# One decoder layer in fp32 on one core: the embedding operand in another order, and its weights' second parts by accumulating transfers

## The chip, the cores and the metric

The kernel runs on one core of one Trainium2 chip. The core has five engines that run side by side: TensorE (PE, with a separate row PEld for its weight loads), VectorE (DVE), ScalarE (ACT), GpSimd (POOL) and SyncE (SP). SP and POOL issue most of the transfers (DMA). What counts is device time in microseconds (us), from three runs.

## The reference

One layer of a decoder works on 512 tokens of width 1024: half a SwiGLU FFN; then a convolution branch and a windowed attention branch that are merged by gates; then the second half FFN; then the embedding stage, which alone the change touches; and a last norm:

```python
    gate = jax.nn.sigmoid(rms_norm(h, g_ple[i]) @ w_ple_gate[i])
    h = h + gate * (p[i] @ w_ple_proj[i])
return rms_norm(h, g_final)
```

`p` is the layer's embedding (512 tokens x 256), `w_ple_proj` is 256 x 1024 and `w_ple_gate` 1024 x 1024. All is fp32.

## The kernel before, in words

**Products in three parts.** TensorE takes fp32 in a rounded form (fp32r). To keep the precision, each operand is split into a high part (rounded) and a low part (what the rounding left), and each product is done as three: high x high, high x low, low x high. So each weight slab exists as `wh` and `wl`.

**How a slab's two parts are made.** There are two ways. Usually SP loads the raw slab (`wr`), ACT casts it into `wh` (L422) and DVE subtracts (`wl = wr - wh`, L423). For slab kinds listed in `POOLED` (L90), POOL loads the slab straight into `wh`, ACT writes its rounded negative into `wl` (L374), and POOL issues a second transfer from the same weights, which adds them to `wl` while it writes (L376). The function `by_dma` chooses, `load_one` loads, `early_one` starts the second transfer, `split_one` does the first way.

**Order.** `slab_order` lists all slabs in the order of their use. `slab(key)` is called at each use; it hands out the slab's parts and, ahead of that, issues loads, sums, second transfers and casts for the slabs behind, so that each engine's instructions stand in a fixed order. SP's and POOL's transfers are issued in that order too, and an instruction that waits holds up all behind it on its engine. Slabs and their parts live in 16 rotating buffers of 128 x 1024; a load waits until its buffer's last reader is done.

**The embedding stage** stands at the end of the program. Its slabs are one `pT` (the embedding, transposed: 128 partitions, two halves of 512 tokens), two `pp` (the projection, 512 KB each) and eight `pg` (the gate's weights, 512 KB each, made in split form by ACT at L413 and DVE at L414). Tokens are handled in four classes, by the remainder of the token's number by 4: class b holds tokens 4i + b. `by_class` is a view that takes every fourth element.

- For each `pp` slab j and each class b, six products (L1591 to L1593) go into one bank, with 128 tokens of pT as the stationary operand and 512 columns of weights moving; ACT copies the bank out (L1595). That is 48 products. Before the last block, TensorE sums the squares for the norm (L586), which DVE's additions (L575) have to finish.
- The gate's products for class 0 (L1607 to L1609) use each `pg` slab as it comes, six products a slab; those of the classes 1 to 3 follow with all slabs at hand.
- `row` (L1576) writes the 1024 gains of the last norm, element by element, into a row in memory, and `gf` (L1579) spreads it over the partitions. Both stand in SP's queue behind the third `pg` load and ahead of the fourth.

Just before this stage, TensorE works off the second FFN's down products (L712 to L715), whose results DVE adds to the residual (L727).

Of the kernel before, what the change touches and what calls it, by code (L numbers as in the profile page):

```python
# [18 lines left out]
P = 128  # L19
S = 512  # L20
# [4 lines left out]
NB = S // P  # L25
# [61 lines left out]
POOL_MIX = False  # L87
POOL_SUMS = False

POOLED = ("win", "v", "ao", "co")  # L90
RAISED = ("dp", "v0")
BY_DMA = ("B11", "B21", "T4")

# [63 lines left out]
def block_kernel(ctx: ExitStack, tc: tile.TileContext, a, out):  # L157
# [22 lines left out]
    def by_class(t):  # L180

        return t.rearrange("p (i c) -> p c i", c=NB)
# [78 lines left out]
    def product(key):  # L261
        return key[2] if key[0] in ("1", "2", "m") else None
# [131 lines left out]
    def split_one():  # L394
        i = state["split"]
        if i in halves:
            state["split"] = i + 1
            return
        r, q, kind = raws.pop(i), product(order[i]), order[i][0]
        if q is not None:  # L400
            w = r.shape[-1]
            h, l = W("wh", F32R)[:, :w], W("wl", F32R)[:, :w]
            spend(0.25 + w * 0.00075, 0.17 + w * 0.001)
            A.activation(h, r, AF.Copy)  # L404
            V.tensor_sub(l, r, h.bitcast(F32))  # L405
            halves[i] = h, l
        elif kind == "pg":
            hs, ls, low = [], [], W("wl", F32R)
            for c in range(2):
                z = r.rearrange("p (m k i) -> p k m i", k=2, i=P)[:, c]  # L410
                h, l = T("pgh", F32R), low[:, c * S:(c + 1) * S]
                hm, lm = (t.rearrange("p (m i) -> p m i", i=P) for t in (h, l))
                A.activation(hm, z, AF.Copy)  # L413
                V.tensor_sub(lm, z, hm.bitcast(F32))  # L414
                hs.append(h)
                ls.append(l)
            halves[i] = (hs, ls)
        else:
            w = r.shape[-1]
            h, l = W("wh", F32R)[:, :w], W("wl", F32R)[:, :w]  # L420
            halves[i] = (h, l)
            A.activation(h, r, AF.Copy)  # L422
            V.tensor_sub(l, r, h.bitcast(F32))  # L423
        state["split"] = i + 1
# [71 lines left out]
    p = bank("warm")  # L496
    for _ in range(N_WARM):
        PE.matmul(p[:, :P], one, one, start=True, stop=True)
    p = None
# [566 lines left out]
    h = x  # L1066
# [65 lines left out]
    for c in range(KD):  # L1132
        z = c, bank("pb"), bank("pa"), T("gg"), T("glu")
# [19 lines left out]
    z = None  # L1153
# [222 lines left out]
    for s in range(NSLOT):  # L1376
        q, k = [], []
        now = Attention(q, k)
        p = bank("pq")
# [3 lines left out]
        p = None  # L1383
# [12 lines left out]
        for g in range(NG):  # L1396
            for base, dst in ((16, q), (28, k)):
                p = bank("pq")
# [7 lines left out]
                p = None  # L1406
# [4 lines left out]
        for j in range(2):  # L1411
            wh, wl = (blocks_of(z, 4) for z in slab(("v", s, j)))
            for kk in range(4):
                for c in range(NB):
                    xh, xl = (classes(z)[:, c] for z in us[4 * j + kk])
# [74 lines left out]
    for base in (48, 40):  # L1490
        for m in range(KD):
            p = bank("pg")
# [17 lines left out]
    for j in range(4):  # L1510
        wh, wl = slab(("ao", j))
        for i in range(2):
            m = 2 * j + i
            p = bank("pb")
            for kk in range(4):
                c = slice((4 * i + kk) * P, (4 * i + kk + 1) * P)
# [8 lines left out]
    for m in range(KD):  # L1525
        p = bank("py")
# [20 lines left out]
    for g in range(2):  # L1547
        ps = {q: bank(q) for q in ("pa", "pe", "pd")}
        for q in MIXED:
# [4 lines left out]
            p = ps[BANKS[q]]  # L1554
# [26 lines left out]
    pTh, pTl = slab(("pT",))  # L1581
    pp = {}
    for j in range(2):
        wh, wl = (z.rearrange("p (i k m) -> p k i m", i=4, k=2) for z in slab(("pp", j)))
        for b in range(NB):
            if j and b == 3:
                r = gnorm.by_token(diag=False)
            p = bank("pp")
            for kk in range(2):
                xh, xl = (by_class(z[:, kk * S:(kk + 1) * S])[:, b] for z in (pTh, pTl))  # L1590
                PE.matmul(p, xh, wh[:, kk], start=kk == 0, stop=False)  # L1591
                PE.matmul(p, xl, wh[:, kk], start=False, stop=False)
                PE.matmul(p, xh, wl[:, kk], start=False, stop=kk == 1)  # L1593
            pp[b, j] = T("pp")
            A.activation(pp[b, j], p, AF.Copy)  # L1595
            for _ in range(min(len(later), 3)):
                next_job(later)
    pTh = pTl = wh = wl = None
# [149 lines left out]
```

## Time and profile before

| | |
|---|---|
| Median of three runs | 1283.06 us (1282.82 to 1283.29) |
| Span of the profiled execution, first to last instruction | 1280.8 us |
| TensorE busy | 1267.4 us (99%) |
| DVE, ACT, POOL busy | 1015.3, 740.9, 299.8 us |
| Transfers | 226.12 MB, mean 177 GB/s |
| First product of the embedding (L1591), of the gate (L1607) | 1210.89 us, 1225.07 us |
| Last matmul of the program | 1271.80 us |

The profile gives times from the span's start; the profiled execution's own device time stands nowhere but in that span, and 2.3 us lie between it and the median. In a row of the timeline stand the start, the duration, the engine, the line, the operation, what is written from what, how many were merged, and in brackets how long the engine sat idle before it and what released it. "SPq" and "POOL ... DMA" rows are issues of transfers; they land later. A row by line has the busy time and the mean duration in ns. A row by stretches has the busy time and the count of PE, PEld, DVE, ACT and POOL, then the granted TensorE clock (1.00 is full), the share of the 16 transfer engines and GB/s. Transfers issued by SP show as queue q1, those by POOL as q0.

### The profile page before, as it was taken

The page shows a single profiled execution, that of the slowest core. Times are in us where ns is not written, and L with a number is a line of the kernel's source. Part 1 is how long each engine was busy: PE and PEld are TensorE (multiplying, and loading weights), DVE is VectorE, ACT ScalarE, POOL GpSimd, SP SyncE. Part 2 cuts the span into 40 slices and gives each one's busy share as a digit, 9 for nine tenths or more (in the row PEclk, how much of TensorE's full clock was granted, in tenths as well). Part 3 has the DMA queues.
Part 4 walks back from the last instruction along what each step waited for, and adds up shares of the span by engine and source line. Part 5 has one row for each costly group of instructions (what it writes and reads, how often), then busy time and mean ns, then how long its engine had stood idle before and what let it go on. Part 6 is the DMA issues. An engine that isn't in the chain of part 4 may idle for free.

```text
span 1280.8 us, 21791 instructions
## 1 busy us (share of the span) xinstructions
PE 1267.4 (99%) x8266; PEld 1163.6 (91%) x8266; DVE 1015.3 (79%) x1617; ACT 740.9 (58%) x1088; POOL 299.8 (23%) x392
## 2 busy tenths in 40 slices
PE   9999999999999999999999999999999999999997
PEld 7899999998988888989898888898899999998986
DVE  6988778898969887878778755786988888786875
ACT  6677566575643264746565445373677566585662
POOL 3122222132223232333232222012122122132000
PEclk9999999999999999999999999999999999999999
DMA  9676876867879889898887788657576876867641
GB/s 302 148 171 161 204 201 157 206 165 191 193 177 227 213 152 204 155 188 150 173 183 166 168 190 218 160 119 211 132 177 159 203 206 146 208 168 187 155 115 50
DMA packets 114128, 226.12 MB, mean 177 GB/s; under 512 B 20584, under 2 KB 50664, under 8 KB 114024
## 3 DMA queue, kind: packets, MB, share of 16 engines
q0 software_dynamic: 49600, 142.10, 54.6%
q1 hardware_dynamic: 64136, 82.37, 20.1%
q8 instruction: 65, 1.06, 0.3%
q14 instruction: 39, 0.32, 0.1%
q10 hardware_dynamic: 288, 0.26, 0.1%
HBM read 168.56 MB, written 2.13 MB: 133 GB/s over the span
## 4 chain that ended last, share of the span: by engine, by line
PE 76%; DVE 2%; issue 0%; ACT 0%; DVEq 0%
PE pa L712 5%; PE pa L713 5%; PE pa L715 5%; PE pq L458 4%; PE pq L459 4%; PE pq L460 4%; PE pg L458 3%; PE pg L460 3%; PE pg L459 3%; PE pd L713 3%; PE pd L715 3%; PE pd L712 3%; PE pb L459 2%; PE pb L460 2%; PE pb L458 2%; PE pe L713 1%
## 5 line engine op out<-in xcount | busy, mean ns | idle before, releaser
L376 POOL DMA_DIRECT2D wl<-wr x108 | 93.4, 867 | 440.4 <-ACT wl L374 341.1
L712 PE MATMUL pa<-bh,wh 128*128 128x256 f32 x680 | 167.6, 284 | 0.5 <-DVE gx L727 0.4
L713 PE MATMUL pa<-bl,wh 128*128 128x256 f32 x680 | 167.3, 283 | 0.0
L1098 DVE SCALAR_TENSOR_TENSOR acc<-glu,taps,acc 128x511 f32<-128x511 f32 (+14 forms) x240 | 161.6, 732 | 0.0
L405 DVE TENSOR_TENSOR wl<-s,wh 128x1024 fp32r<-128x1024 f32 (+1 forms) x96 | 108.5, 1132 | 38.0 <-ACT wh L404 37.8
L374 ACT ACTIVATE wl<-wh 128x1024 fp32r<-128x1024 f32 x84 | 87.9, 1051 | 81.9 <-DMA wh<-in_w_in 50.8
L712 PEld LDWEIGHTS pa<-bh,wh 128*128 128x128 f32 x680 | 130.6, 192 | 1.0 <-issue 0.5
L713 PEld LDWEIGHTS pa<-bl,wh 128*128 128x128 f32 x680 | 130.8, 192 | 0.0
L374 ACT ACTIVATE wl<-wr 128x1024 fp32r<-128x1024 f32 (+1 forms) x108 | 105.7, 979 | 24.3 <-DVE wl L405 11.4
L404 ACT ACTIVATE wh<-s 128x1024 fp32r<-128x1024 f32 (+1 forms) x96 | 93.0, 969 | 38.8 <-PE pd L459 14.7
L388 ACT ACTIVATE wh<-wr 128x1024 fp32r<-128x1024 f32 (+1 forms) x108 | 105.5, 977 | 11.0 <-PE pd L715 6.1
L712 PE MATMUL pd<-bh,wh 128*128 128x256 f32 x448 | 110.3, 284 | 0.0
L713 PE MATMUL pd<-bl,wh 128*128 128x256 f32 x448 | 110.2, 283 | 0.0
L376 POOL DMA_DIRECT2D wl<-in_w_in x56 | 48.5, 869 | 219.6 <-ACT wl L374 200.5
L715 PE MATMUL pa<-bh,wl 128*128 128x256 f32 x680 | 97.0, 283 | 0.0
L458 PE MATMUL pq<-xsh,wh 128*128 128x512 f32 x224 | 88.8, 396 | 0.0
L715 PEld LDWEIGHTS pa<-bh,wl 128*128 128x128 f32 x680 | 88.4, 192 | 0.0
L459 PE MATMUL pq<-xsl,wh 128*128 128x512 f32 x224 | 87.4, 390 | 0.0
L460 PE MATMUL pq<-xsh,wl 128*128 128x512 f32 x224 | 87.4, 390 | 0.0
L713 PEld LDWEIGHTS pd<-bl,wh 128*128 128x128 f32 x448 | 86.2, 192 | 0.0
L712 PEld LDWEIGHTS pd<-bh,wh 128*128 128x128 f32 x448 | 86.1, 192 | 0.1
L458 PE MATMUL pg<-xsh,wh 128*128 128x512 f32 x192 | 76.1, 396 | 0.2 <-ACT xsh L478 0.2
(330 smaller groups left out, 3616.0 us busy)
## 6 DMA issues: line engine op xcount, KB each, us to landing
wl<-wr POOLq DMA_DIRECT2D x72, 512.0 KB, 5.7
wh<-in_w_in POOLq DMA_DIRECT2D x56, 512.0 KB, 7.0
wl<-in_w_in POOLq DMA_DIRECT2D x56, 512.0 KB, 6.0
wr<-in_w_ffn_up SPq DMA_DIRECT2D x80, 256.0 KB, 4.4
wr<-in_w_ffn_gate SPq DMA_DIRECT2D x78, 256.0 KB, 4.8
wr<-in_w_ffn_down SPq DMA_DIRECT2D x96, 192.0 KB, 3.8
wl<-wr POOLq DMA_DIRECT2D x36, 384.0 KB, 4.4
wr<-in_w_ffn_down SPq DMA_DIRECT2D x16, 256.0 KB, 4.1
```

Of the source, the lines that this page charges most:

```text
L374: A.activation(l.bitcast(F32R), h, AF.Copy, scale=-1.0)
L376: G.dma_start(to, src, accum_op=OP.add)
L388: A.activation(h, r, AF.Copy)
L404: A.activation(h, r, AF.Copy)
L405: V.tensor_sub(l, r, h.bitcast(F32))
L458: PE.matmul(ps, wh, xh, start=start, stop=False, skip_group_check=part)
L459: PE.matmul(ps, wh, xl, start=False, stop=False, skip_group_check=part)
L460: PE.matmul(ps, wl, xh, start=False, stop=stop, skip_group_check=part)
L712: PE.matmul(o, h[:, c], th, start=q in ("B11", "B21", "T1") and i == 0, stop=False, skip_group_check=True)
L713: PE.matmul(o, h[:, c], tl, start=False, stop=False, skip_group_check=True)
L715: PE.matmul(o, l[:, c], th, start=False, stop=i >= len(at) - 2, skip_group_check=True)
L1098: bg.append(lambda acc=acc, g=g, w=w, s=s: V.scalar_tensor_tensor(acc[:, s:], g[:, :S - s], w, acc[:, s:], op0=OP.mult, op1=OP.add))
```

## The change

Two things are done. When pT is split, both of its parts are written class by class: the cast (L422 before, L425 after) and the subtraction (L423, L426) read every fourth element and write neighbours, and the products then take 128 neighbouring columns as the stationary operand. And the kind "pp" joins `POOLED`: its two slabs are made in the second of the two ways above.

```diff
-POOLED = ("win", "v", "ao", "co")
+POOLED = ("win", "v", "ao", "co", "pp")
...
             halves[i] = (h, l)
+            if kind == "pT":
+                r = r.rearrange("p (k i c) -> p k c i", k=2, c=NB)
+                h, l = (z.rearrange("p (k c i) -> p k c i", k=2, c=NB) for z in (h, l))
             A.activation(h, r, AF.Copy)
             V.tensor_sub(l, r, h.bitcast(F32))
...
             for kk in range(2):
-                xh, xl = (by_class(z[:, kk * S:(kk + 1) * S])[:, b] for z in (pTh, pTl))
+                xh, xl = (z[:, kk * S + b * P:kk * S + (b + 1) * P] for z in (pTh, pTl))
```

Lines behind the second place move by three (L1591 becomes L1594).

POOL's last transfers, behind the second FFN's (wl<-wr):

```order
 L376 DMA wl_12943<-wr_12843 128x768
 L376 DMA wl_13027<-wr_12808 128x768
-L1744 UNCONDITIONAL_BRANCH
-L1744 ISA
+L273 DMA wh_13059<-in_w_ple_proj 128x1024
+L273 DMA wh_13088<-in_w_ple_proj 128x1024
+L376 DMA wl_13142<-in_w_ple_proj 128x1024
+L376 DMA wl_13172<-in_w_ple_proj 128x1024
+L1747 UNCONDITIONAL_BRANCH
+L1747 ISA
```

POOL had nothing behind the second FFN; it now issues two plain loads and two accumulating ones.

ACT, from pT's cast to the first pg cast, before (wh_13138 is pT's high part, wh_13169 and wh_13200 are the projection's, sq are squares for the norm):

```order
L422 ACTIVATE wh_13138<-wr_12998 128x1024
L567 ACTIVATE sq_13163<-h_3928 128x512
L567 ACTIVATE sq_13166<-h_3929 128x512
L422 ACTIVATE wh_13169<-wr_13059 128x1024
L422 ACTIVATE wh_13200<-wr_13088 128x1024
L413 ACTIVATE pgh_13211<-wr_13113 128x512
```

and now:

```order
L425 ACTIVATE wh_13138<-wr_12998 128x1024
L374 ACTIVATE wl_13142<-wh_13059 128x1024
L570 ACTIVATE sq_13166<-h_3928 128x512
L570 ACTIVATE sq_13169<-h_3929 128x512
L374 ACTIVATE wl_13172<-wh_13088 128x1024
L413 ACTIVATE pgh_13209<-wr_13113 128x512
```

The first projection slab's operation now stands ahead of the two squares, the second's behind them; both are negations.

DVE, at the same place (gx and h are the residual), before:

```order
L423 TENSOR_TENSOR wl_13139<-wr_12998,wh_13138 128x1024
L727 SCALAR_TENSOR_TENSOR gx<-pd_12993,gx 128x2x256
L575 TENSOR_TENSOR sq_13134<-sq_13134,sq_13136 128x512
L575 TENSOR_TENSOR sq_13134<-sq_13134,sq_13163 128x512
L423 TENSOR_TENSOR wl_13170<-wr_13059,wh_13169 128x1024
L727 SCALAR_TENSOR_TENSOR gx<-pa_12991,gx 128x2x256
L423 TENSOR_TENSOR wl_13201<-wr_13088,wh_13200 128x1024
L414 TENSOR_TENSOR wl_13210<-wr_13113,pgh_13211 128x512
```

and now:

```order
L426 TENSOR_TENSOR wl_13139<-wr_12998,wh_13138 128x1024
L730 SCALAR_TENSOR_TENSOR gx<-pd_12993,gx 128x2x256
L578 TENSOR_TENSOR sq_13134<-sq_13134,sq_13136 128x512
L578 TENSOR_TENSOR sq_13134<-sq_13134,sq_13166 128x512
L730 SCALAR_TENSOR_TENSOR gx<-pa_12991,gx 128x2x256
L414 TENSOR_TENSOR wl_13208<-wr_13113,pgh_13209 128x512
```

The two subtractions for the projection are gone. On SP the two loads of the projection are gone as well, and pT is followed by the first three pg loads, row, the two gf and the last five pg loads, in that order as before; the second pg load goes into another buffer.

## The prediction

> **What bounds the kernel now.** I read the page's first two parts, then the waits, and then the stage that the change touches, by engine, in order of time. The page says how full TensorE is:
>
> ```profile
> span 1280.8 us, 21791 instructions
> PE 1267.4 (99%) x8266; PEld 1163.6 (91%) x8266; DVE 1015.3 (79%) x1617; ACT 740.9 (58%) x1088; POOL 299.8 (23%) x392
> ```
>
> TensorE sets the end. A change is worth what it takes from TensorE's own time or its stalls, and costs what it makes TensorE wait. From 1190 us on, the waits name one stall of TensorE only, on a DVE subtraction of L423; the timeline shows it in the embedding's products (L1591 to L1593, of 48):
>
> ```profile
> 1211.23 0.40 PE L1592 MATMUL pp<-wh,wl 128*128 128x512 f32 x1
> 1212.21 0.63 PE L1593 MATMUL pp<-wl,wh 128*128 128x512 f32 x1 [0.58 <-DVE wl L423]
> 1212.67 0.40 PE L1591 MATMUL pp<-wh,wh 128*128 128x512 f32 x1
> ...
> 1221.60 0.40 PE L1593 MATMUL pp<-wl,wh 128*128 128x512 f32 x1
> ...
> 1225.07 0.47 PE L1607 MATMUL pg<-pgh,xsh 128*128 128x512 f32 x1
> ...
> 1235.85 0.39 PE L1609 MATMUL pg<-wl,xsh 128*128 128x512 f32 x1
> ```
>
> Undisturbed, a product of this stage starts every (1221.60 - 1212.67) / 38 = 0.235 us. So L1591, which stands at 1212.67, was due at 1211.23 + 2 x 0.235 = 1211.70: the stall costs 0.97 us. The gate's products behind it (L1607 to L1609) start every (1235.85 - 1225.07) / 47 = 0.229 us.
>
> Next I read SP, whose queue brings the gate's eight slabs (pg):
>
> ```profile
> 1201.72 3.39 SPq L273 DMA_DIRECT2D wr<-in_w_ple_gate  x3
> 1205.16 0.82 SPq L1576 DMA_DIRECT2D row<-in_gx  x1
> 1218.99 0.82 SPq L1579 DMA_DIRECT2D gf<-row  x2
> 1219.92 5.35 SPq L273 DMA_DIRECT2D wr<-in_w_ple_gate  x5
> ```
>
> Three pg loads go out, then a transfer of 1024 single elements (row), and then SP stands for 13 us until row has landed. The last five pg loads are queued behind that. Two stretches of it, with the transfers' share and GB/s in the last two columns:
>
> ```profile
> 1204.00:1208.40 4.40, 4.40 (x39) 4.40 (x39) 3.59 (x5) 3.61 (x6) 0.00 (x0) 1.00 0.99 332
> ...
> 1211.00:1218.90 7.90, 7.32 (x31) 7.01 (x31) 7.73 (x12) 5.33 (x10) 0.00 (x0) 1.00 0.00 0
> ```
>
> The three pg loads fill the transfer engines (0.99). Row comes behind them on the same ring and then lands slowly with the engines empty (0.00): its tail does not hang on bandwidth, but its start hangs on the pg loads ahead of it. The last five pg loads arrive just ahead of their use:
>
> ```profile
> 1226.63 1.16 ACT L413 ACTIVATE pgh<-wr 128x512 fp32r<-128x512 f32 x2 [0.52 <-DMA wr<-in_w_ple_gate]
> ...
> 1232.52 1.15 ACT L413 ACTIVATE pgh<-wr 128x512 fp32r<-128x512 f32 x2 [0.23 <-DMA wr<-in_w_ple_gate]
> 1231.80 2.67 DVE L414 TENSOR_TENSOR wl<-wr,pgh 128x512 fp32r<-128x512 f32 x4 [0.20 <-ACT pgh L413]
> ```
>
> ACT waits for each slab's landing, and the last slab's second part is ready at 1231.80 + 2.67 = 1234.47, while its last product starts at 1235.85. Less 0.1 us from the write to the product, the **slack of the whole chain from row to the last pg product is 1.3 us**.
>
> **The change, part by part.** *The order of pT.* The two halves of pT are written class by class, so TensorE reads 128 neighbours where it read every fourth element. The weight loads of both kinds, and the two engines' strided operations elsewhere, are:
>
> ```profile
> L1592 PEld LDWEIGHTS pp<-wh,wl 128*128 128x128 f32 x16 | 5.0, 313 | 0.0
> ...
> L1608 PEld LDWEIGHTS pg<-pgh,xsl 128*128 128x128 f32 x16 | 3.0, 188 | 0.6
> L1103 ACT ACTIVATE cv<-acc x8: 581/598/600, 433.5 to 731.6; 128x512 f32<-128x512 f32 x8
> L1128 DVE TENSOR_TENSOR glu<-pa,gg x8: 1060/1066/1076, 373.7 to 437.9; 128x512 f32<-128x512 f32 x8
> 1207.38 1.22 DVE L423 TENSOR_TENSOR wl<-wr,wh 128x1024 fp32r<-128x1024 f32 x1
> ```
>
> A load falls from 313 to 188 ns, but most of it lies under the product before it. What shows is the step, 0.235 to 0.229: 48 x 0.006 = 0.3 us gained. The rounding now reads with a step of four. ACT's strided copy (598 ns for 512 columns) takes no longer than its plain casts of that size (1.16 us for two, above), so this costs nothing. DVE's strided form takes 1066 ns where plain ones take 2.67 / 4 = 0.67 us; at that ratio the subtraction of pT takes 1.9 us instead of the 1.22 of the row at 1207.38. It would end at 1209.3, ahead of its use at 1211.23, and DVE loses two subtractions of that length just behind it. Without this cover the cost would be 0.7 us.
>
> The Trainium skill ("SBUF — State Buffer", section "Door 1: The DMA port swizzle") says that fp32 accesses a 16-byte line apart each pay, which fits the 313 against 188 ns; by it ACT's read of pT would pay as well, where this trace's strided copy shows no penalty. By the page the sum would not move, since pT's rounding is ahead of its use.
>
> *The weights' second parts.* SP loses two loads of 512 KB. POOL gets four: two loads straight into wh, and two accumulating ones into wl, each behind an ACT negation (L374), which stands for the cast that is gone. DVE loses two subtractions. When do the second parts land, and what do they meet?
>
> ```profile
> 1202.45 1.06 ACT L422 ACTIVATE wh<-wr 128x1024 fp32r<-128x1024 f32 x1 [0.38 <-PE pa L715]
> wl<-in_w_in POOLq DMA_DIRECT2D x56, 512.0 KB, 6.0
> DMA to landing us min/median/max: 3.9/5.5/11.2
> ```
>
> pT's cast starts at 1202.45 as before; the first negation follows it directly, 1203.5 to 1204.5. POOL issues at 1204.6, and by the median 6.0 us of the same kind of transfer it lands at 1210.6 (bounds 3.9 to 11.2: 1208.5 to 1215.8). TensorE needs it at 1211.23 + 0.235 = 1211.5. I take the median: no stall, 0.97 gained. The second negation stands behind two squares, so its transfer goes out near 1206.7 and lands by 1213; its first use is four blocks later, near 1217.
>
> TensorE would so be 0.97 + 0.25 us earlier at the sums of squares (42 of the 48 products lie ahead), which it reached at 1221.60 + 0.24. DVE's additions for them end at 1217.82 + 3.87 = 1221.69 by the row
>
> ```profile
> 1217.82 3.87 DVE L575 TENSOR_TENSOR sq<-sq,sq 128x512 f32<-128x512 f32 x5
> ```
>
> and move by 0.97 only, since ACT's squares hang on the first block's copy: 0.1 to 0.2 us is lost there. TensorE reaches the gate's products about **1.1 us earlier**, at 1224.0.
>
> Against this stands the traffic. What two queues do to each other is seen where accumulating transfers (q0) run alone (1165 to 1167 us; columns are packets, MB and share):
>
> ```profile
> q0 software_dynamic: 120, 0.43, 107.8%
> ```
>
> where they run beside SP's queue q1 (1159 to 1161 us):
>
> ```profile
> q0 software_dynamic: 86, 0.35, 87.9%
> q1 hardware_dynamic: 72, 0.11, 16.9%
> ```
>
> and where q1 runs alone, with the pg loads (1206 to 1208 us):
>
> ```profile
> q1 hardware_dynamic: 715, 0.71, 102.1%
> ```
>
> Alone, accumulating moves 0.43 MB in 2 us, 213 GB/s. Beside it, q1 keeps some 72 packets in 2 us where it has 715 alone: the queues take turns packet by packet, and the accumulating packets are long. Two second parts, 1.05 MB, take 1.05 / 213 GB/s = 4.9 us of all transfer engines. They start near 1206, when two of the three pg loads and row are still to go, and these are pushed back by what lies between: all 4.9 us, unless the second comes after the pg loads are through (then 2.5). The lower bound is 0. Plain loads moved from SP to POOL change nothing here; their bytes pass before 1204 either way. The second pg load also gets another buffer, which is free one down product later than the first load's, some 2 us after 1201.72; the first load's own bytes take 0.52 MB / 332 GB/s = 1.6 us of it.
>
> Row starts 4.9 us later, lands that much later (its tail is its own), and SP releases gf and the last five pg loads at 1223.9. The last second part is ready at 1234.47 + 4.9 = 1239.4, 4.9 - 1.3 = **3.6 us** past its use. TensorE's 1.1 us are lost in that wait. The profiled execution becomes 1280.8 + 3.6 = 1284.4; 2.3 us lie between its span and the median of the runs, 1283.06, so the forecast is 1283.06 + 3.6 = **1286.7 us**.
>
> **The rivals.**
> *The clock falls in the stall.* TensorE would have nothing from 1224.0 + 3 x 1.37 = 1228.1 (three slabs) until the fourth slab's cast at 1226.63 + 0.6 + 4.9 = 1232.1, 4 us. After the last product the clock column shows:
>
> ```profile
> 1271.80 0.28 PE L1609 MATMUL pg<-wl,xsh 128*128 128x256 f32 x1
> 1274.00:1275.00 1.00, 0.00 (x0) 0.00 (x0) 0.74 (x4) 0.12 (x2) 0.00 (x0) 0.96 0.00 0
> 1275.00:1276.00 1.00, 0.00 (x0) 0.00 (x0) 0.86 (x4) 0.00 (x0) 0.00 (x0) 0.50 0.00 0
> ```
>
> 0.96 is 0.08 us at half clock, so it fell 2.8 us after the last product ended. Two slabs at half clock cost 2 x 1.37 more, less what the transfers' pace (1232.52 - 1226.63) / 4 = 1.47 us a slab leaves: some 1.5 to 2.3 us on top, 1288.2 to 1289. Against it: no idle time inside the kernel shows it. The Trainium skill ("TensorE: Matmul & The Clock Gate", "What's actually happening") has the clock halve after an idle window of about 3.4 us that runs freely; by that a 4 us gap need not hold one.
>
> *One second part meets the pg loads, not both*: 2.5 - 1.3 = 1.2 us, 1284.2. It needs the second negation to wait for a late load; against it, both loads pass with little else in their way.
>
> *The second parts hide* (the other side): row is not pushed, and TensorE keeps its 1.1 us: 1281.9. This decides if row still lands by 1219 + 1.3 - 1.1. For it: 0.00 share after 1211. Against it: 0.99 just when they start.
>
> *The second part comes too late for TensorE*: at the bound 1215.8, 4.3 us of stall for the 0.97 removed, +3.0 after the weight loads' 0.3, 1286.1, with the pg chain hidden under it.
>
> **How the numbers follow.** Forecast 0.40 (1285.8 to 1287.5 by itself), clock 0.18, one of two 0.22, hidden 0.15, late 0.05. What this measurement can tell from no change is 0.2%, 2.6 us: slower means over 1285.6, faster under 1280.5. Slower takes the forecast, the clock and half of the late case: 0.60. Faster would need more than the 1.3 us that TensorE has to give: 0.02. The rest is 0.38. The range runs from the hidden case to the clock case, 1281.8 to 1288.7.
>
> **What would show it.** Right: gf issued near 1224 instead of 1218.99, ACT's casts of the last five slabs waiting for their landing 5 us later, a TensorE wait of about 4 us at the fourth pg slab, no wait at pp, weight loads of pp at 188 ns. Wrong: gf still at 1219, or q1 moving at several hundred packets in 2 us beside the accumulating transfers; then the time is 1282.

## The result, and the profile after

The changed kernel takes 1295.59 us (median; 1293.76 to 1296.38), beside 1282.94 us (1282.71 to 1283.29) for the kernel before, measured with it: a ratio of 1.0095, with an interval from 1.0082 to 1.0108. It is slower by 12.65 us, where 3.6 had been forecast.

The page of the changed kernel, its first two lines of numbers: TensorE's own busy time went up by 3.8 us and the span by 13.8. The profiled execution is the longest of the four that the median comes from.

```profile
span 1294.6 us, 21793 instructions
PE 1271.2 (98%) x8266; PEld 1163.3 (90%) x8266; DVE 1014.3 (78%) x1615; ACT 742.1 (57%) x1088; POOL 303.0 (23%) x396
```

The changed kernel's waits of TensorE from 1190 us on (in total, times, longest) show two stalls where there was one of 0.6 us. The one forecast, at the fourth gate slab, is the small one:

```profile
PE pp L1596 <- DMA wl<-in_w_ple_proj: 8.3, 1, 8.3
PE pg L1610 <- ACT pgh L413: 1.6, 1, 1.6
```

TensorE's timeline places them (the lines moved by three: L1594 to L1596 are the projection's products, L1610 to L1612 the gate's):

```profile
1211.75 0.40 PE L1595 MATMUL pp<-wh,wl 128*128 128x512 f32 x1
1220.45 0.80 PE L1596 MATMUL pp<-wl,wh 128*128 128x512 f32 x1 [8.30 <-DMA wl<-in_w_ple_proj]
...
1234.51 0.48 PE L1610 MATMUL pg<-pgh,xsh 128*128 128x512 f32 x1
...
1238.47 0.39 PE L1612 MATMUL pg<-wl,xsh 128*128 128x512 f32 x1
1240.46 0.50 PE L1610 MATMUL pg<-pgh,xsh 128*128 128x512 f32 x1 [1.60 <-ACT pgh L413]
...
1249.05 0.39 PE L1612 MATMUL pg<-wl,xsh 128*128 128x512 f32 x1
```

Laid beside the same rows of before, from the second product of the projection to the last of the gate's first class, the stage takes 1249.05 - 1211.75 = 37.30 us instead of 1235.85 - 1211.23 = 24.62. Of these 12.7 us:

- Second product to third: 8.70 instead of 0.98, **7.7 us**.
- Third product to the gate's first: 14.06 instead of 12.86, **1.2 us**.
- The gate's first product to the last of class 0: 14.54 instead of 10.78, **3.8 us**; 1240.46 - 1238.47 - 0.23 = 1.8 of it is the second stall.

Another 0.5 us was there already at 1211.75 (the kernels measured below, the kernel before among them, reach this product between 1211.07 and 1211.95), and 0.6 us follow the stage.

The second and third parts need the clock. Stretches of the changed kernel, with the busy time and count of PE, PEld, DVE, ACT and POOL, then the granted clock, the transfers' share and GB/s:

```profile
1211.00:1214.00 3.00, 1.15 (x8) 0.71 (x6) 2.76 (x5) 0.00 (x0) 0.00 (x0) 1.00 1.91 154
1214.00:1220.00 6.00, 0.00 (x0) 0.00 (x0) 0.00 (x0) 0.00 (x0) 0.00 (x0) 0.50 0.93 30
1220.00:1224.30 4.30, 3.85 (x9) 3.08 (x10) 0.50 (x1) 1.74 (x4) 0.00 (x0) 0.50 0.56 87
...
1240.00:1246.00 6.00, 5.54 (x16) 4.12 (x17) 4.94 (x8) 4.69 (x9) 0.00 (x0) 0.72 0.86 271
```

The clock is at half from 1214 to 1224.3 and once more after the second stall, so the products behind each stall start every 0.43 us instead of 0.23 for a while. The last two columns are the other news: from 1214 to 1220 the transfer engines are as good as busy (0.93) and move 30 GB/s, where the forecast had reckoned with 213.

Why the second part is late shows in two rows, of ACT and of POOL. The cast of pT takes 2.11 us where it took 1.06, and POOL's first accumulating transfer goes out at 1206.43, not at 1204.6:

```profile
1203.08 2.11 ACT L425 ACTIVATE wh<-wr 128x1024 fp32r<-128x1024 f32 x1 [0.38 <-PE pa L718]
1206.43 0.87 POOL L376 DMA_DIRECT2D wl<-in_w_ple_proj  x1 [4.61 <-ACT wl L374]
```

Then it takes far longer to land than the 6.0 us taken for it. The queues from 1206 to 1210 us (packets, MB, share of the 16 engines) with the transfers issued there (the last number is the median from issue to landing), and the queues from 1214 to 1216:

```profile
q1 hardware_dynamic: 1081, 1.06, 85.9%
q0 software_dynamic: 6, 0.01, 1.3%
...
wl<-in_w_ple_proj POOLq DMA_DIRECT2D x2, 512.0 KB, 14.7
...
q0 software_dynamic: 15, 0.05, 80.3%
q1 hardware_dynamic: 8, 0.00, 2.7%
```

Up to 1210 the gate loads have the engines almost to themselves; the accumulating packets come only when these are through. After that, from 1214 to 1216, fifteen packets hold 80.3% of 16 engines for 2 us, 25.7 us in all: 1.7 us a packet. Where the accumulating queue ran alone before (the prediction's row of 120 packets at 107.8%) a packet took 0.29 us.

The chain of waits, lastly, read back from the end of class 0, does not go through the long stall at all. It goes through row:

```profile
1205.79 25.77 DMA row<-in_gx
1231.58 0.35 SPq L1582
...
1232.52 7.23 DMA wr<-in_w_ple_gate
1239.77 0.64 ACT pgh L413
1240.46 0.50 PE pg L1610
```

Row took 25.8 us from its issue to its landing, where it took 1218.99 - 1205.16 = 13.8 in the kernel before. Its packets on q1 tell where the time went. In the kernel before the last of its elements is recorded by 1211, and it lands 8 us behind that. In the changed kernel some 500 elements pass by 1212, few in the next 10 us, and 440 packets, most of the rest, only from 1222 to 1224, when the accumulating packets run out (q1 from 1212 to 1222 and from 1222 to 1224):

```profile
q1 hardware_dynamic: 83, 0.00, 7.9%
...
q1 hardware_dynamic: 440, 0.00, 13.9%
```

The last element is recorded at 1224.05, and row lands 7.5 us behind that. So its tail is as long as it was; its elements were held up.

So two paths are late at once: TensorE's own, over the second part, which would have reached the fourth gate slab at 1238.7, and row's, which made that slab ready at 1240.46.

### The profile page after: what moved, and what is told of

It is laid out like the page before. It is cut to its first block, busy times and chain, and to the rows that moved or that the text cites. A ratio compares the mean times of both kernels' runs of the same rounds, so it can differ in the third digit from the quotient of the medians.

```text
span 1294.6 us, 21793 instructions
## 1 busy us (share of the span) xinstructions
PE 1271.2 (98%) x8266; PEld 1163.3 (90%) x8266; DVE 1014.3 (78%) x1615; ACT 742.1 (57%) x1088; POOL 303.0 (23%) x396
## 3 DMA queue, kind: packets, MB, share of 16 engines
q8 instruction: 65, 1.06, 0.3%
## 4 chain that ended last, share of the span: by engine, by line
PE 71%; DVE 3%; DMA 3%; issue 1%; ACT 0%; SPq 0%; DVEq 0%
PE pa L715 5%; PE pa L718 5%; PE pa L716 5%; PE pq L461 4%; PE pq L462 4%; PE pq L463 4%; PE pg L461 3%; PE pg L463 3%; PE pg L462 3%; PE pd L716 2%; PE pd L715 2%; PE pd L718 2%; DMA row<-in_gx 2%; PE pb L462 2%; PE pb L461 2%; PE pb L463 2%
```

## The experiments

My theory before the runs: row's writes of single elements and the accumulating packets hold each other up; the stepped cast decides that they meet. The main rivals: the bytes alone count (second parts against gate loads), the classes' order itself costs, or the half clock is the loss. All runs in one table. "Landing" is the median from issue to landing of the accumulating transfers, "SP for row" is SP's wait on row, "stall" is TensorE's longest wait at the projection, all from one execution, the profiled one; the last column is the ratio to the kernel before on the same chip. In two kernels that execution lies 3 us from the median: with half of row it is the fastest (1292.89 us, the others 1295.78 to 1295.95), with pT laid out the slowest (1292.68, the others 1287.33 to 1291.16).

| Kernel | Median, us | Stall | Landing | SP for row | Ratio (interval) |
|---|---|---|---|---|---|
| Before | 1282.94 to 1283.27 | 0.6 | none | 12.9 | |
| Changed | 1295.59 | 8.3 | 14.7 | 25.0 | 1.0095 (1.0082 to 1.0108) |
| Order of pT only | 1283.39 | 1.1 | none | 12.2 | 1.0001 (0.9992 to 1.0010) |
| Second parts only | 1287.90 | 2.1 | 9.0 | 18.7 | 1.0037 (1.0024 to 1.0050) |
| Changed, no row | 1288.49 | 4.2 | 10.2 | none | 1.0039 (1.0027 to 1.0052) |
| Before, no row | 1283.20 | 0.6 | none | none | 1.0000 (0.9992 to 1.0009) |
| Changed, half of row | 1295.82 | 8.6 | 14.9 | 21.0 | 1.0093 (1.0078 to 1.0108) |
| Changed, clock kept up | 1296.27 | 1.6 | 15.9 | 25.5 | 1.0102 (1.0085 to 1.0119) |
| Changed, one second part | 1290.97 | 5.6 | 15.9 | 13.3 | 1.0060 (1.0045 to 1.0075) |
| Changed, pT laid out | 1289.66 | 2.2 | 9.2 | 20.3 | 1.0052 (1.0034 to 1.0070) |
| the same, 1 us late | 1294.97 | 8.4 | 16.3 | 24.6 | 1.0092 (1.0078 to 1.0106) |
| Changed, row behind | 1287.46 | 1.8 | 7.7 | 18.5 | 1.0036 (1.0022 to 1.0049) |
| Changed, pT laid out, no row | 1286.83 | 3.1 | 10.0 | none | 1.0029 (1.0018 to 1.0040) |
| Changed, row in 128 pieces | 1285.04 | 2.6 | 8.4 | 7.8 | 1.0015 (1.0006 to 1.0025) |
| Changed, no row, clock kept up | 1286.14 | 0.5 | 10.7 | none | 1.0025 (1.0015 to 1.0034) |
| Candidate | 1282.60 | none | none | 12.2 | 0.9996 (0.9987 to 1.0005) |

### Each half of the change alone

The order of pT only, with "pp" left out of `POOLED`:

```diff
-POOLED = ("win", "v", "ao", "co", "pp")
+POOLED = ("win", "v", "ao", "co")
```

> pT in class order, but the projection's second parts by DVE as before (no accumulating transfers added). Theory A (the accumulating transfers and the one-element row hold each other up on the transfer engines; the order of pT is harmless): the 48 products gain 0.3 us, the DVE stall at the third product stays near 1 us, 1282.6 us. Rival C (the cast of pT, 2.1 us in the profile after instead of 1.06, makes everything behind it late): TensorE waits longer at the embedding's products, 1284 us or more.

Measured: 1283.39, no change; it lies between the two expectations. The 0.3 us of the shorter product step are not to be had, since DVE pays for the order. In this kernel's DVE rows the stepped subtraction takes 2.06 us, where 1.9 had been forecast, and TensorE's wait for the slab's second part grows from 0.6 to 1.1:

```profile
1207.33 2.06 DVE L426 TENSOR_TENSOR wl<-wr,wh 128x1024 fp32r<-128x1024 f32 x1
...
PE pp L1596 <- DVE wl L426: 1.1, 1, 1.1
```

The second parts only: "pp" in `POOLED`, pT and its reading as before.

> The projection's second parts by accumulating transfers, pT in the old order (cast of 1.06 us). Theory A, and rival B (the second parts and the pg loads just fill the transfer engines): nearly the whole loss is here, 1293.5 to 1296.5 us, with the first second part landing 12 us or more after its issue. Rival C: under 1290 us, since the second part is issued 1 us earlier.

Measured: 1287.90, so 4.8 us slower, not 10 to 13: rival C's figure, and not my theory's. The order of pT alone costs nothing, the second parts alone 4.8, both together 12.65: the two halves act on each other. The only thing by which the order of pT can reach the second parts is ACT's cast. Here that takes 1.06 us, and the issue by POOL comes 1.5 us earlier than in the changed kernel (0.45 of it because this execution reaches the cast that much earlier):

```profile
1204.94 0.87 POOL L376 DMA_DIRECT2D wl<-in_w_ple_proj  x1 [3.56 <-ACT wl L374]
...
PE pp L1593 <- DMA wl<-in_w_ple_proj: 2.1, 1, 2.1
```

### Without row

The gains are laid out as one row in memory beforehand, and `gf` reads that; the same was done to the kernel before.

```diff
-    row, gf = dram.tile([1, D], F32, name="row"), [T("gf") for _ in range(2)]
-    nc.sync.dma_start(row.rearrange("o (c p e) -> o c p e", c=KD, e=1), bass.AP(
...
+    gf = [T("gf") for _ in range(2)]
...
-        nc.sync.dma_start(gf[c], row[0:1, c * S:(c + 1) * S].partition_broadcast(P))
+        nc.sync.dma_start(gf[c], a["gf"][0:1, c * S:(c + 1) * S].partition_broadcast(P))
```

> The changed kernel, with the last norm's gains taken from a row that the host has laid out, so that the 1024-element transfer is gone; gf is still spread over the partitions at its place in SP's queue. Theory A: the second parts land 5 to 8 us after their issue, the wait at the third product is under 1.5 us, the last five pg loads come some 13 us earlier, no fall of the clock, 1281.5 to 1282.5 us. Rival B: the second parts still meet three pg loads, they land 10 us or more after their issue and TensorE waits 4 us or more, 1287 us or more.

> The kernel before, with the gains taken from the laid-out row. All theories: row hides there (slack of 1.3 us behind it, nothing else on the queues), so within 0.4 us of 1283.0. If it is faster by 1 us or more, row costs something by itself and the comparison of the run above has to be made against this one.

Measured: 1288.49 and 1283.20. The first is rival B's figure; my theory's 1281.5 to 1282.5 is missed by 6 us, so row is not the whole loss. Row costs the kernel before nothing, and taking it from the changed kernel gives back 7.1 us, about as much as undoing the order of pT. What is left, 5.4 us, comes with a landing of 10.2 us instead of the median 6.0 that the prediction used, now that all eight gate loads go out early, and with the half clock behind the stall of 4.2 us (priced below). Where both are taken away (pT laid out in classes in memory, so that no cast reads with a step, and no row), 1286.83:

> The changed kernel with pT laid out in the tokens' classes in memory and the gains laid out as one row, so that neither the stepped copy nor the transfer of single elements is left; both second parts by accumulating transfers. Theory (the stepped copy's lateness and row are two separate prices): against the changed kernel without row (1288.5) the first second part is issued 1.05 us earlier, TensorE's wait falls from 4.2 to 2.2 to 3.2 us, and the time is 1286.5 to 1287.5. Rival (without row the lateness costs nothing, the gate loads alone set the landing): 1288 to 1289.

By the medians that is 1.7 us less than without row alone, for a cast that is 1.05 us shorter (the two intervals overlap); the stall is 1.1 us shorter. With no row, nothing tips over.

### Which comes first

Does being late by 1 us cost 1 us, or does it change what the second part meets? The changed kernel with pT laid out in the classes' order, so that ACT's cast is plain and 1.06 us long:

```diff
-            if kind == "pT":
-                r = r.rearrange("p (k i c) -> p k c i", k=2, c=NB)
-                h, l = (z.rearrange("p (k c i) -> p k c i", k=2, c=NB) for z in (h, l))
...
-    f["pT"] = np.ascontiguousarray(g["p"][0, 0].T.reshape(2, P, S).transpose(1, 0, 2)).reshape(P, 2 * S)
+    f["pT"] = np.ascontiguousarray(g["p"][0, 0].T.reshape(2, P, P, NB).transpose(1, 0, 3, 2)).reshape(P, 2 * S)
```

> The changed kernel with pT laid out in the tokens' classes in memory, so that ScalarE's and VectorE's rounding reads it without a step of 4; both second parts by accumulating transfers, row as it was. Theory (the stepped copy made the second parts 1.05 to 1.5 us late, and that is 7.7 of the 12.6 us): the rounding takes 1.06 us on ScalarE, the first second part is issued before 1205.2, TensorE's wait is 2 to 3.5 us, and the time is 1287.0 to 1288.5 as with the second parts alone, less 0.3. Rival (the lateness is no part of it, the classes' order itself is): 1293.5 to 1296.5.

And this kernel with nothing but ACT's negation of the first slab done twice:

```diff
+                if order[i] == ("pp", 0):
+                    A.activation(l.bitcast(F32R), h.bitcast(F32), AF.Copy, scale=-1.0)
                 remainder(l, h.bitcast(F32), sources(order[i]))
```

> The kernel with pT laid out in the classes' order (1289.7), with ScalarE's negation of the first projection slab done twice, so that the first second part is issued some 1.05 us later, as in the changed kernel, and nothing else is altered. Theory (it decides which of the two comes to the transfer engines first, row's single elements or the accumulating packets): issued at 1206.3 to 1206.6, accumulating packets of about 2 us instead of 0.33, a wait of 7 to 9 us, and 1294 to 1296.5. Rival (a delay of one microsecond costs one microsecond): 1290 to 1291.5.

Measured: 1289.66 (1287.33 to 1292.68, wider than any other and above the expectation) and 1294.97. In the kernel with pT laid out, the stall and the accumulating queue from 1212 to 1214 us:

```profile
PE pp L1593 <- DMA wl<-in_w_ple_proj: 2.2, 1, 2.2
...
q0 software_dynamic: 112, 0.39, 99.5%
```

In the one with the doubled negation, the stall, the queue from 1212 to 1214 and the same from 1216 to 1218:

```profile
PE pp L1595 <- DMA wl<-in_w_ple_proj: 8.4, 1, 8.4
...
q0 software_dynamic: 63, 0.22, 151.0%
...
q0 software_dynamic: 21, 0.08, 113.5%
```

99.5% of 16 engines over 2 us are 31.8 us for 112 packets, 0.28 us each; in the late kernel 36.3 us go to 21 packets, 1.7 us each. The order of issue shows what the microsecond changed. In the kernel with pT laid out POOL issues the first second part at 1205.37, 0.4 us ahead of row (1205.78); with the negation doubled, at 1206.09, 0.7 us behind row (1205.41). In the kernel with the second parts only it is again 0.4 us ahead (1204.94 and 1205.34), and its packets are fast too.

By the medians, one microsecond of lateness cost 5.3 us. The classes' order itself, which both kernels have, is not what parts them. What switches is how long a packet takes; how much time that costs is less sure. The two profiled executions lie only 1.5 us apart (1292.68 and 1294.13): in the first one row was late all the same (SP waited 20.3 us), and TensorE stood still for 3.2 us more at the fourth gate slab. Why this kernel's runs spread so widely is open.

The reverse: the changed kernel, late as it is, but row issued by POOL behind the two second parts.

```diff
-    nc.sync.dma_start(row.rearrange("o (c p e) -> o c p e", c=KD, e=1), bass.AP(
+    nc.gpsimd.dma_start(row.rearrange("o (c p e) -> o c p e", c=KD, e=1), bass.AP(
```

> The changed kernel with the transfer row issued by GpSimd behind the two second parts instead of by SyncE ahead of them; all else as it was. Theory (accumulating packets are slow only where row's single elements have come first): accumulating packets of 0.33 us, TensorE's wait 2.5 to 4.5 us, row landing 1222 to 1227, time 1287 to 1291. Rival (in whichever order, sharing the engines costs the same): 1294 to 1297.

Measured: 1287.46, inside the theory's range of times (the wait, 1.8 us, is shorter than it said). Here the accumulating transfers land 7.7 us after their issue, at 108.1% x 32 us / 120 = 0.29 us a packet, and row, behind them, takes 15.3. The transfers issued from 1205 to 1210, the accumulating queue from 1212 to 1214, and TensorE's waits:

```profile
wl<-in_w_ple_proj POOLq DMA_DIRECT2D x2, 512.0 KB, 7.7
...
row<-in_gx POOLq DMA_DIRECT2D x1, 4.0 KB, 15.3
...
q0 software_dynamic: 120, 0.43, 108.1%
...
PE pg L1610 <- ACT pgh L413: 2.6, 1, 2.6
PE pp L1596 <- DMA wl<-in_w_ple_proj: 1.8, 1, 1.8
```

So accumulating packets are slow where row's single elements have come ahead of them, and not where these come behind. This run alone would not show it, for it alters more than the order: issued by POOL, row stands in the trace as 32 packets of 256 bytes, at 1214.9 to 1216.3, and not as 1024 of 4. But in the kernels with pT laid out and with the second parts only, SP issues row in its old form just behind the first second part, and there the packets are fast as well.

### How much of row it takes

> The changed kernel with the transfer `row` cut to 512 of its 1024 single elements; both halves of the gains are then read from the same 512, so half of the gains are left out. Theory (row's writes of 4 bytes and the accumulating transfers hold each other up, packet by packet, and row's late landing sets the end): row lands some 5 to 6 us earlier than 1231.4, TensorE's wait at the first second part shrinks from 8.3 us to 5 to 6.5, and the time falls from 1295.6 to 1288.5 to 1291. Rival (only the bytes count, and row has 4 KB of them): waits as in the changed kernel, 1294.5 to 1296.

```diff
-    row, gf = dram.tile([1, D], F32, name="row"), [T("gf") for _ in range(2)]
+    row, gf = dram.tile([1, S], F32, name="row"), [T("gf") for _ in range(2)]
```

(The transfers' ranges follow.) Measured: 1295.82, as with all of row and as the rival had it; the stall is 8.6 us. The theory's number was missed: half as many elements do not slow the packets half as long. That it is not the bytes either, the run with 128 pieces below shows.

> The changed kernel with only the second projection slab's second part by an accumulating transfer; VectorE subtracts the first's. TensorE then waits about 1.1 us at the first slab (as with the order alone), and one transfer of 4.9 us for two stands beside row. Theory (row is what the accumulating packets hold up): row lands at 1222 to 1227 and the time is 1285 to 1289. Rival (the wait for the first slab's second part was the whole loss, row and gate loads have slack): 1283 to 1284.

```diff
-POOLED = ("win", "v", "ao", "co", "pp")
+POOLED = ("win", "v", "ao", "co")
...
-        return product(key) in BY_DMA or key[0] in POOLED + RAISED or key[0] == "gq" and key[2] > 0
+        return product(key) in BY_DMA or key == ("pp", 1) or key[0] in POOLED + RAISED or key[0] == "gq" and key[2] > 0
```

(`load_one` likewise.) Measured: 1290.97, above both expectations, and for another reason than row's lateness: SP waits for row 13.3 us, as in the kernel before, but the one accumulating transfer takes 15.9 us, with a stall of 5.6 us at the second slab. The queues of this kernel from 1210 to 1212 and from 1212 to 1214 show it most plainly:

```profile
q0 software_dynamic: 26, 0.11, 182.0%
q1 hardware_dynamic: 783, 0.05, 33.6%
...
q0 software_dynamic: 13, 0.05, 76.3%
q1 hardware_dynamic: 7, 0.00, 0.2%
```

By 1212 the records of row's elements are through (783 packets of q1 in these 2 us, most of them row's); in the next 2 us hardly one is left, and still 13 accumulating packets take 76.3% x 32 / 13 = 1.9 us each. Row has landed only at 1221.03. So the packets are slow in the time between row's last record and its landing, and not because its packets share an engine's time with them. I had put the mutual hold-up down to the latter. Row itself is not late here: its elements had passed before the accumulating packets could hold them up.

The last of this group writes the same gains in 128 pieces of eight neighbours:

```diff
-    nc.sync.dma_start(row.rearrange("o (c p e) -> o c p e", c=KD, e=1), bass.AP(
-        tensor=a["gx"].tensor, offset=a["gx"].offset + V_GF, ap=[[0, 1], [1, KD], [V_DW + S, P], [1, 1]]))
+    nc.sync.dma_start(row.rearrange("o (p c) -> o p c", c=KD), bass.AP(
+        tensor=a["gx"].tensor, offset=a["gx"].offset + V_GF, ap=[[0, 1], [V_DW + S, P], [1, KD]]))
```

> The changed kernel with the transfer row cut into 128 pieces of eight neighbouring elements (32 bytes) instead of 1024 single elements; the gains then stand in another order than the computation wants. Halving the number of single elements had shortened nothing. Theory (any short writes that are still under way slow the accumulating packets, whatever their number): packets of about 2 us again, a wait of 6 to 9 us, 1292 to 1296.5. Rival (it is the single elements, 1024 or 512 of them): accumulating packets of 0.33 us, a wait of 2 to 4 us, 1286 to 1289.

Measured: 1285.04, below both ranges, with packets and a wait as the rival had them. Its waits of SP and TensorE, and the accumulating queue from 1212 to 1214:

```profile
SPq L1582 <- DMA row<-in_gx: 7.8, 1, 7.8
...
PE pp L1596 <- DMA wl<-in_w_ple_proj: 2.6, 1, 2.6
...
q0 software_dynamic: 117, 0.42, 105.6%
```

Row is ahead of the second parts as it was, and the packets take 0.29 us. So neither the 4 KB nor row's place ahead makes the trouble by itself, but the cutting into single elements does: 512 or 1024 pieces of 4 bytes slow the accumulating packets five to eight times, 128 pieces of 32 bytes do not. Whether number or size decides between 128 and 512 pieces was not tried, nor whether it is the reading of single elements or the writing, since the pieces are the same on both sides. No run shows why they slow an accumulating packet. The Trainium skill ("DMA: Bandwidth & Descriptors", section "Specifications") says that transfers below 512 bytes are done by reading, altering and writing; that would fit slow single elements, but the pieces of 32 bytes lie below it as well and were harmless.

### What the clock costs

> The changed kernel with 32 products nobody reads ahead of the third product of the projection (7.3 us at 0.227 us each, in its wait of 8.3) and 14 ahead of the fourth gate slab, so that TensorE does not stand still and its clock should stay at 1. If row's late landing sets when the fourth gate slab is there (1240.46 us), the half clock after the first wait (1.9 us) lies beside it and only the half clock after 1241.34 (1.7 us) comes back: 1293.9 (1293.4 to 1294.4). If TensorE's own path sets the end and both count: 1292.0 (1291.5 to 1292.6). If the half clock is none of the loss: 1295.3 to 1296.5.

```diff
+                if j == b == kk == 0:
+                    d = bank("fill")
+                    for _ in range(32):
+                        PE.matmul(d, xh, wh[:, kk], start=True, stop=True)
+                    d = None
                 PE.matmul(p, xh, wl[:, kk], start=False, stop=kk == 1)
```

(And 14 at the gate.) Measured: 1296.27, no gain, against all but the last of the expectations. The clock did stay up, as the stretches of this kernel from 1214 to 1217 and from 1240 to 1246 show, and TensorE waited only 1.6 and 1.0 us outside the filling:

```profile
1214.00:1217.00 3.00, 3.00 (x15) 2.46 (x14) 0.00 (x0) 0.00 (x0) 0.00 (x0) 1.00 1.14 31
...
1240.00:1246.00 6.00, 5.05 (x20) 3.20 (x19) 3.88 (x6) 4.10 (x8) 0.00 (x0) 1.00 1.00 325
...
PE pp L1601 <- DMA wl<-in_w_ple_proj: 1.6, 1, 1.6
PE pg L1615 <- ACT pgh L413: 1.0, 1, 1.0
```

The half clock behind the long stall is thus none of the loss: row's path sets when the fourth gate slab starts. Of the half clock behind the second stall this run can't say so. Here SP issued the last five gate loads only from 1235.34 us on, against 1232.52, because the second gf's issue took 3.15 us instead of 0.43, and the fourth slab starts at 1241.56, 1.1 us later than in the changed kernel (1240.46). From there to the end of the span it takes 52.9 us instead of 54.1. So the full clock gained some 1.2 us and the late issue took them; whether the filling has to do with that issue is open. Where there is no row, the same filling (18 products) tells the clock's own price:

> The changed kernel without row (gains laid out, 1288.5), with 18 products nobody reads ahead of the third product of the projection, in TensorE's wait of 4.2 us, so that the clock stays up. No transfer follows from row here, so TensorE's own path sets the end. If products at half clock are a price by themselves: twelve products took 4.83 us from 1216.35 us where they take 2.75 at full clock, so 2.1 us come back, 1286.4 (1285.8 to 1287.0). If the end is set by something else again: 1288 to 1289.

Measured: 1286.14 against 1288.49, 2.35 us by the medians, close to the 2.1 worked out. The clock stays at 1.00 from 1212 to 1224, where it is at 0.50 from 1215 to 1220 without the filling. The two were measured on different chips, and the intervals of their ratios overlap; but no run of the one lies within those of the other. The half clock after a stall of 4.2 us is a price by itself where TensorE's own path sets the end.

### A candidate

The kernel before, with pT laid out in classes in memory and the two subtractions for the projection on POOL, which is idle there:

```diff
-            V.tensor_sub(l, r, h.bitcast(F32))
+            (G if kind == "pp" else V).tensor_sub(l, r, h.bitcast(F32))
```

> A candidate made from the kernel before: pT laid out in the classes' order in memory, no accumulating transfers for the projection, and the two slabs' second parts subtracted by GpSimd, which is idle there, instead of by VectorE. If GpSimd takes four times its 0.94 us for 128x256, the first second part is there at about 1209.5, ahead of the third product, and the wait of 1 us and the 0.3 us of product step go: 1281.5 to 1282.1. If its subtraction is there only after 1211.5: 1283 to 1285.

Measured: 1282.60, between the two expectations, a ratio of 0.9996 with an interval from 0.9987 to 1.0005: no difference that can be told. The wait at the projection is gone, POOL taking 3 us for each subtraction, but another has taken its place, at the sums of squares (waits of TensorE, then POOL's row):

```profile
PE ss L586 <- DVE sq L575: 0.6, 1, 0.6
...
1205.84 6.01 POOL L423 TENSOR_TENSOR wl<-wr,wh 128x1024 fp32r<-128x1024 f32 x2 [7.98 <-ACT wh L422]
```

DVE's additions, of which the prediction had said that they move by less than TensorE gains, are the next bound. No version tried here beats the kernel before.

## Why the prediction was right in direction and wrong in size

**The product step** was right as a step: at full clock the changed kernel's weight loads of the projection take 188 ns (its row in the stretch from 1225 to 1231 us below), as forecast. A product's step is (1231.20 - 1224.60) / 29 = 0.228 us, from the starts of two of its products. The order alone shows, though, that the 0.3 us do not reach the end.

```profile
L1595 PEld LDWEIGHTS pp<-wh,wl 128*128 128x128 f32 x9 | 1.7, 188 | 0.3
```

**DVE's stepped subtraction** came out at 2.06 us for the forecast 1.9, partly by luck: the row it was worked out from (L1128) writes with a step and reads neighbours, while the subtraction of pT reads with a step and writes neighbours.

**ACT's stepped rounding "costs nothing"** was wrong, and it is the step on which most hangs. I took L1103, a stepped copy of 512 columns at 598 ns, for the likeness of the cast of pT; that cast takes 2.11 us instead of 1.06. The page of the Trainium skill cited in the prediction ("SBUF — State Buffer", "Door 1: The DMA port swizzle") had ACT's read of pT pay, and the measurement sides with it. The prediction then said that by the page the sum would not move, since pT's rounding is ahead of its use. That looked at pT's use alone. The negation that starts the first second part is queued behind this cast on ACT, so the 1.05 us went straight into the issue by POOL. It put row ahead of the second part. The doubled negation shows what such a microsecond costs: 5.3 us by the medians.

**The landing at 1210.6** was wrong twice. The issue came at 1206.43 instead of 1204.6; 1.05 us of that is the cast, 0.6 us this execution's later start. And the landing took 14 us where the range of all such transfers in the kernel before ended at 11.2. That range came from stages without a transfer like row. The nearest in the kernel before are transfers in 512 pieces of 8 bytes (`st<-own`, `other<-st`, from 472 to 686 us), and behind one of them, from 562 to 564 us, stands a sign that was passed over:

```profile
q0 software_dynamic: 14, 0.06, 37.9%
```

These packets take 37.9% x 32 / 14 = 0.87 us each instead of 0.29. The landings of that stage still ended at 9.2 us. So the range was taken as a bound, and was none.

**"No stall, 0.97 gained"** fell with it: a stall of 8.3 us.

**"Pushed back all 4.9 us"** failed in what is pushed and by how much. The gate loads were not pushed at all (1081 packets against 6 up to 1210); by the prediction's own sign of being wrong, q1 moving at several hundred packets, the time should then have been 1282. The 72 packets that it had gone by stand in a stretch where SP issued one load of 192 KB. What was pushed was row: its way from issue to landing grew by 12 us. "Its tail is its own" held, 7.5 us against 8 behind the last element. But the elements were not 4.9 us late, a figure worked out from bytes. Some 500 of them passed, the accumulating packets became slow, and most of the rest waited until these were done. With row in 128 pieces the loss is 1.8 us, with row behind 4.3, and the forecast had 3.6; that they lie near it is luck, for with 128 pieces the stall is one of 2.6 us at the projection and none at the gate.

**The chain from row over gf to the fourth gate slab** was right in its links and its order: SP released gf and five gate loads when row had landed, ACT waited for the slab, TensorE for ACT. It was late by 12.6 us instead of 4.9, and is what the chain of waits names.

**The rivals.** *The clock falls in the stall* came true, at a stall that I had not foreseen (at the projection) as well as at the one I had. Its price in the kernel without row, 2.35 us behind a stall of 4.2, lies just above the 1.5 to 2.3 worked out for the other stall. I had doubted a fall even in a gap of 4 us, and it came in shorter ones: behind the second stall of 1.6 us above, and behind the stall of 2.1 us in the kernel with the second parts only, while it stayed at full behind 2.6 us where row is in 128 pieces (stretches of these two kernels, the clock before the last two columns):

```profile
1214.00:1217.00 3.00, 3.00 (x8) 2.48 (x9) 0.00 (x0) 1.12 (x3) 0.00 (x0) 0.58 0.63 90
```

```profile
1214.00:1216.00 2.00, 1.51 (x7) 1.24 (x7) 0.00 (x0) 0.26 (x1) 0.00 (x0) 1.00 0.86 202
```

The length of the gap alone does not decide, nor need the clock fall in the gap: behind the stall of 1.6 us it reads 0.83 over 1240 to 1242, which is half clock for 0.7 us, so it fell at 1241.3, when TensorE had been at work again for 0.9 us. The Trainium skill ("TensorE: Matmul & The Clock Gate", "What's actually happening") has the clock halve after an idle window of some 3.4 us; the stalls of 1.6 and 2.1 us do not hold such a window, and the measurement decides. *One second part meets the pg loads, not both* did not come about; hardly a packet of either met them. *The second part comes too late for TensorE* was nearest in kind; its price (+3.0) was bound by the same 11.2 us. *The second parts hide* was wrong in every variant: with the cast plain and no row, the time is 3.7 us above that of before, and the best of them, row in 128 pieces, is still 1.8 above.

What the forecast lacked was not another rival but the case in which the late second part and the delayed row come together: each had its price by itself, and the two were taken to lie side by side.

## What to carry to other kernels

A cheap instruction that moves ahead of an issue on the same engine is to be priced at that issue and not at its own result's use: here 1 us more on ACT cost some 5 us by the medians, because it changed which of two transfers came first. A transfer of hundreds of single elements that seems to land on idle engines can still slow others until it has landed; keep accumulating transfers out of that time, issue it behind them, or cut it into longer pieces. And a range of landing times holds for the company in which it was measured.

## What the runs showed of the hardware that had not been expected

- Behind 1024 or 512 single elements of 4 bytes, accumulating packets took some 1.4 to 2.5 us each instead of 0.28 to 0.29, for 5 us in the changed kernel (1213 to 1218) and 8 with one second part (1210 to 1218), also after the last record of such an element; 128 pieces of 32 bytes did not do this. The elements in turn, where about half had passed, waited for the accumulating packets. The same 4 KB landed in 8.4 us in 128 pieces, accumulating transfers beside them, and in 13.8 us as 1024 single elements in the kernel before, with none.
- The granted clock fell behind stalls of 1.6 and 2.1 us and not behind one of 2.6 us. In the changed kernel the fall of 1241.3 came 0.9 us after the stall had ended.
- ACT's cast of 128 x 1024 from fp32 read with a step of four elements took 2.11 us instead of 1.06, and DVE's subtraction 2.06 instead of 1.22, while a stepped copy of 128 x 512 elsewhere (L1103) took no longer than a plain one. Why that one does not pay was not tried.
